# Two model blocks on one core: the scheduler's simulation is exchanged, and with it the order of every engine

## The chip, the cores and the metric

The kernel runs on one core of a Trainium2 chip. The metric is the device time of one execution in microseconds (us). Runs of this kernel scatter by about 0.2%. Engines are named as in the profile: PE is TensorE (PEld its weight loads), DVE is VectorE, ACT is ScalarE, POOL is GpSimd, SP is the engine that issues the loads.

## What is computed

Two transformer-like blocks on 512 tokens of width 1024, in float32. The first block (one layer) mixes by three branches: gated linear attention (GLA, 4 heads, chunked), a causal convolution, and attention in a window of 128 tokens with sinks (8 heads); then an FFN with a convolution. The second block has two layers, each with top-128 sparse attention (8 heads), an HGRN recurrence (4 heads), two gates and an FFN. Cut to the second block's mix:

```python
for l in range(DEPTH_2):
    h = rmsnorm_2(x, norm_mix[l])
    proj = h @ w_in[l]
    aq, ak, av, iq, ik, iw, hq, hf, hi, hg, ga, gb = jnp.split(proj, split_points, axis=-1)
    ...
    y_attn = dsa_attention(aq, ak, av, iq, ik, iw)     # scores of an indexer, top 128, softmax over these
    ...
    o = hgrn2_chunked(q_h, k_in, v_h, log_f)           # S_t = diag(f_t) S_{t-1} + k_t v_t^T
    ...
    merged = jax.nn.sigmoid(ga) * (y_attn @ w_proj_attn[l]) + jax.nn.sigmoid(gb) * (y_hgrn @ w_proj_hgrn[l])
    x = x + merged @ w_out[l]
    h = rmsnorm_2(x, norm_ffn[l])
    g, u = jnp.split(h @ w_ffn_in[l], 2, axis=-1)
    x = x + (jax.nn.silu(g) * u) @ w_ffn_out[l]
```

## The kernel before, in words

Activations lie with features on the 128 partitions and the 512 tokens along the row. A projection (`project`, L184) multiplies one 128-column tile of a weight with all eight tiles of the input: each float32 product is made of three matmuls of high and low parts (L193 low weight, L194 low input, L195 both high), so a projection of 1024 inputs is 24 matmuls of 512 columns into one PSUM bank. `project_tokens` (L156) does the same with tokens on the partitions (L168 to L170). The weights come through `weights` (L133): SP loads 512 KB into `wraw` (three buffers), ACT rounds the high part (`whi`, L149), and DVE or POOL subtracts it (`wlo`, L152).

The second block's mix (`second_mix`, L957) first does the sparse attention (`dsa`, L828): an indexer's scores, for query blocks 1 to 3 a selection of the 128 best by 16 rounds of MAX8 and MATCH_REPLACE8 on DVE (L885, L886), normalised and rotated keys and queries (`rotated`, L818, whose last multiplication is L825, followed by transposes on PE at L239 and, for queries, two copies at L249), and then `attend` (L915) for four query blocks of 128 tokens, eight heads each. A head is: scores on PE (L925, up to 512 columns), bias and minimum on DVE (L927), exp on ACT (L929), up to four transposes on PE (L933), a copy on ACT (L935), up to four matmuls with the values on PE (L937). At the end of a block the output is normalised (L941) and transposed. The scores and transposes use PSUM banks of lane "a"; that lane has two, and one of them holds the output `o` of the query block. Behind the attention in program order come four HGRN heads (`hgrn_head`, L468), each with three projections and seven levels in which DVE (L493, L497) and POOL (L494, L495) take turns and PE multiplies small blocks (L509), and then the two merges (`merge`, L677), whose projections need gates and the mixed outputs. At most two gates are made ahead of the first merge.

No order is written out by hand beyond that of the program. A scheduler takes the whole traced program, simulates the engines, and lets each engine take, at the simulated time at which it is free, the ready instruction of highest priority; weights and PSUM evictions are marked as of high priority. The order that comes out is fixed in the program: on the chip each engine works through its list and waits at semaphores. The scheduler has two simulations to choose from; the default is used before.

## Time and profile before

| | |
|---|---|
| median of 3 runs | 2590.12 us (2587.59 to 2593.46) |
| profiled execution | 2592.11 us |
| its span, first to last instruction | 2590.3 us |
| mean granted clock of PE | 0.990 |
| PE busy | 2504.4 us (97%) |
| DVE, ACT, POOL busy | 1362.4, 1011.7, 769.8 us |
| read from HBM | 213.5 MB, 83 GB/s over the span |

PE's busy time is that of its matmuls, which overlap one another in the pipeline: the mean duration of one 512-column matmul is about 0.39 us, but a run of them goes on at one per 0.227 us. A float32 matmul without the split shows as two rows. The granted clock is 1.00 (2.4 GHz) or 0.50 (1.2 GHz) at any moment; a stretch shows the mean.

### The profile page before, as it was taken

How to read it: one execution, taken by the hardware profiler on the slowest of the kernel's cores; microseconds unless marked ns; L12 is line 12 of the kernel's file. 1: busy time of each engine (PE TensorE's matmuls, PEld its weight loads, DVE VectorE, ACT ScalarE, POOL GpSimd, SP SyncE). 2: the span in 40 equal slices, each digit the busy share in tenths (PEclk: the TensorE clock that was granted, in tenths of full speed). 3: DMA queues.
4: the chain of work that ended last, by engine and by line, in shares of the span. 5: the costliest groups of instructions: out<-in, count | busy, mean ns of one | idle time of the engine just before them, and what ended most of it. 6: DMA issues, size and time to landing. Idle time of an engine off the chain costs nothing.

```text
span 2590.3 us, 31616 instructions
## 1 busy us (share of the span) xinstructions
PE 2504.4 (97%) x11742; PEld 2047.2 (79%) x11742; DVE 1362.4 (53%) x2568; ACT 1011.7 (39%) x1830; POOL 769.8 (30%) x676
## 2 busy tenths in 40 slices
PE   9999999999999998899999999999798999999999
PEld 7877888888888766777888888887677788888887
DVE  4675222477764677765244444336877523444432
ACT  5633333444443344453343333334355333433322
POOL 4234334511101333643361110013465335211100
PEclk9999999999999999999999999999899999999999
DMA  4112233322233222111332223332211123222233
GB/s 136 58 60 82 87 97 98 102 98 98 97 95 96 76 74 73 42 37 59 94 99 98 97 94 95 94 98 66 73 42 40 34 96 101 96 94 96 97 108 88
DMA packets 67434, 217.66 MB, mean 84 GB/s; under 512 B 7744, under 2 KB 8640, under 8 KB 67280
## 3 DMA queue, kind: packets, MB, share of 16 engines
q1 hardware_dynamic: 67280, 215.65, 26.1%
q8 instruction: 92, 1.51, 0.2%
q14 instruction: 62, 0.51, 0.1%
HBM read 213.52 MB, written 2.10 MB: 83 GB/s over the span
## 4 chain that ended last, share of the span: by engine, by line
PE 80%; DVE 14%; POOL 3%; issue 2%; ACT 1%; DMA 0%; SPq 0%; DVEq 0%; POOLq 0%; ACTq 0%
PE mm L194 23%; PE mm L195 23%; PE mm L193 23%; DVE score L886 2%; DVE m L885 2%; PE at L925 1%; PE at L937 1%; PE at L239 1%; DVE wlo L152 1%; POOL hG L495 1%; PE mm L169 1%; PE mm L170 1%; PE mm L168 1%; DVE rsq_w L231 1%; PE at L933 1%
## 5 line engine op out<-in xcount | busy, mean ns | idle before, releaser
L149 ACT CAST whi<-wraw 128x512 fp32r<-128x512 f32 (+3 forms) x824 | 502.3, 610 | 1139.9 <-PE mm L195 950.4
L193 PE MATMUL mm<-xh,wlo 128*128 128x512 f32 x1920 | 759.0, 395 | 0.0
L194 PE MATMUL mm<-xl,whi 128*128 128x512 f32 x1920 | 758.2, 395 | 0.0
L195 PE MATMUL mm<-xh,whi 128*128 128x512 f32 x1920 | 755.5, 393 | 0.0
L152 DVE TENSOR_TENSOR wlo<-wraw,whi 128x512 fp32r<-128x512 f32 (+1 forms) x529 | 385.2, 728 | 458.5 <-ACT whi L149 455.4
L152 POOL TENSOR_TENSOR wlo<-wraw,whi 128x512 fp32r<-128x512 f32 (+2 forms) x295 | 381.4, 1293 | 760.5 <-ACT whi L149 689.6
L195 PEld LDWEIGHTS mm<-xh,whi 128*128 128x128 f32 x1920 | 361.8, 188 | 74.5 <-issue 1.9
L194 PEld LDWEIGHTS mm<-xl,whi 128*128 128x128 f32 x1920 | 361.9, 188 | 73.5 <-issue 1.7
L193 PEld LDWEIGHTS mm<-xh,wlo 128*128 128x128 f32 x1920 | 361.8, 188 | 72.9 <-issue 1.2
L193 PE MATMUL mm<-acth,wlo 128*128 128x512 f32 x528 | 205.4, 389 | 0.0
L194 PE MATMUL mm<-actl,whi 128*128 128x512 f32 x528 | 205.4, 389 | 0.0
L195 PE MATMUL mm<-acth,whi 128*128 128x512 f32 x528 | 205.4, 389 | 0.0
L733 POOL TENSOR_TENSOR fg<-fg,rstd 128x512 f32<-128x512 f32 x44 | 56.7, 1289 | 425.6 <-ACT fg L732 425.6
L168 PE MATMUL mm<-wlo,xh 128*128 128x512 f32 (+2 forms) x384 | 147.0, 383 | 17.3 <-POOL wlo L152 9.2
L169 PE MATMUL mm<-whi,xl 128*128 128x512 f32 (+2 forms) x384 | 145.2, 378 | 0.2 <-DVE xl L288 0.2
L170 PE MATMUL mm<-whi,xh 128*128 128x512 f32 (+2 forms) x384 | 145.1, 379 | 0.0
L202 DVE TENSOR_TENSOR gate<-mm,rstd 128x512 f32<-128x512 f32 x56 | 38.7, 691 | 165.2 <-PE mm L195 164.3
L277 POOL TENSOR_TENSOR acc<-acc,sq 128x512 f32<-128x512 f32 x39 | 58.9, 1509 | 199.2 <-ACT sq L274 198.3
L194 PEld LDWEIGHTS mm<-actl,whi 128*128 128x128 f32 x528 | 99.1, 188 | 20.8
L193 PEld LDWEIGHTS mm<-acth,wlo 128*128 128x128 f32 x528 | 99.1, 188 | 20.6
L195 PEld LDWEIGHTS mm<-acth,whi 128*128 128x128 f32 x528 | 99.1, 188 | 20.4
L168 PEld LDWEIGHTS mm<-wlo,xh 128*128 128x128 f32 x384 | 73.4, 191 | 36.1 <-POOL wlo L152 11.7
(352 smaller groups left out, 3333.1 us busy)
## 6 DMA issues: line engine op xcount, KB each, us to landing
wraw<-in_w_ffn_in SPq DMA_DIRECT2D x88, 512.0 KB, 3.3
wraw<-in_w_gate SPq DMA_DIRECT2D x56, 512.0 KB, 3.3
wraw<-in_w_in SPq DMA_DIRECT2D x52, 512.0 KB, 3.3
wraw<-in_w_up SPq DMA_DIRECT2D x44, 512.0 KB, 3.2
wraw<-in_w_tok SPq DMA_DIRECT2D x32, 512.0 KB, 3.2
wraw<-in_w_ffn_out SPq DMA_DIRECT2D x32, 512.0 KB, 3.6
wraw<-in_w_down SPq DMA_DIRECT2D x16, 512.0 KB, 3.6
wraw<-in_w_po SPq DMA_DIRECT2D x32, 256.0 KB, 2.6
```

The source lines that it names most:

```text
L149: nc.scalar.copy(wh, raw[:, k:k + m, :])
L152: eng.tensor_tensor(wl, raw[:, k:k + m, :], wh.bitcast(F32), op=OP.subtract)
L168: nc.tensor.matmul(ps[t][:, 0:w], xh, wl, start=i == 0, stop=False)
L169: nc.tensor.matmul(ps[t][:, 0:w], xl, wh, start=False, stop=False)
L170: nc.tensor.matmul(ps[t][:, 0:w], xh, wh, start=False, stop=i == KD - 1)
L193: nc.tensor.matmul(ps, wl, xh, start=i == 0, stop=False)
L194: nc.tensor.matmul(ps, wh, xl, start=False, stop=False)
L195: nc.tensor.matmul(ps, wh, xh, start=False, stop=i == n - 1)
L277: (nc.vector if d % 2 and len(acc) > 1 else nc.gpsimd).tensor_tensor(a, a, sq, op=OP.add)
L733: nc.gpsimd.tensor_tensor(g, g, self.rstd, op=OP.mult)
L885: nc.vector.max(m8, sc[:, 0:w])
L886: nc.vector.match_replace(sc[:, 0:w], m8, sc[:, 0:w], TAKEN)
```

## The change

One argument of the context in which the program is traced. With it the scheduler takes ready and free times from the toolchain's other simulation of the engines, and nothing else is different: the operations, the tiles, the buffers and the priorities stay.

```diff
@@ -1097,7 +1097,7 @@
     out = nc.dram_tensor("out_0", (KD, P, T), F32, kind="ExternalOutput").ap()
-    with tile.TileContext(nc) as tc:
+    with tile.TileContext(nc, schedule_with_timeline_sim=True) as tc:
         model(tc, A, out)
```

Of PE's 10,973 instructions, DVE's 2,474, POOL's 681 and SP's 470, the same number of each line stand in both orders; ACT has 30 table loads where it had 36. What moves shows best at the following places.

PE in the last query block of the first layer's attention in the second block. Before, projections (L193 to L195) and HGRN steps (L474, L488) stand between the steps of the heads:

```order
L933 MATMUL at<-csts,aL 128x128 x4
L195 MATMUL mm<-xh,whi 128x512
L193 MATMUL mm<-xh,wlo 128x512
L194 MATMUL mm<-xl,whi 128x512
L195 MATMUL mm<-xh,whi 128x512
L937 MATMUL at<-av,aPT 128x64 x4
L925 MATMUL at<-kT,qT 128x512
L474 MATMUL at<-hq,hk 128x128 x4
L488 MATMUL at<-lvx,ones 128x256
L193 MATMUL mm<-xh,wlo 128x512
L194 MATMUL mm<-xl,whi 128x512
```

At the same place now, from the end of query block 2 on:

```order
L937 MATMUL at<-av,aPT 128x64 x3
L239 MATMUL at<-csts,aon 128x128 x4
L239 MATMUL at<-csts,aro 128x128 x4
L925 MATMUL at<-kT,qT 128x512
L933 MATMUL at<-csts,aL 128x128 x4
L937 MATMUL at<-av,aPT 128x64 x4
L925 MATMUL at<-kT,qT 128x512
```

The three rows L925, L933 and L937 stand there eight times in a row, once for each head, and nothing else between them. From the third head of query block 1 to the end of block 3 PE's list holds 280 instructions and no projection; before, the longest such run is 25 instructions. The second layer has the same run of 280, and the first block's mix has one of 92, where the old order has at most 22.

DVE at the rotated keys in the same layer (aro; akss and rsq are the keys' normalisation, score and m the selection, tabS the rotation's table). Before, the multiplications L825 stand after 16 rounds of the selection at 256 columns and 13 at 384:

```order
L886 MATCH_REPLACE score<-m_7701,score 128x384
L232 SCALAR_TENSOR_TENSOR rsq_w<-rsq_w,rsq_y 128x32
L801 TENSOR_TENSOR rope_8019<-akx,tabS 128x8x32
L885 MAX m_7704<-score 128x8
L233 SCALAR_TENSOR_TENSOR rsq_y<-rsq_w,rsq_y 128x32
L886 MATCH_REPLACE score<-m_7704,score 128x384
L825 TENSOR_TENSOR aro<-aro,rsq_y 128x512
L885 MAX m_7707<-score 128x8
```

Now they stand together, after 16 rounds at 256 columns and 2 at 384:

```order
L886 MATCH_REPLACE score<-m_7671,score 128x384
L233 SCALAR_TENSOR_TENSOR rsq_y<-rsq_w,rsq_y 128x32
L885 MAX m_7674<-score 128x8
L825 TENSOR_TENSOR aro<-aro,rsq_y 128x512 x4
L886 MATCH_REPLACE score<-m_7674,score 128x384
```

At the first attention head of this layer, PE's list has six projection matmuls ahead of the first scores and eleven behind in the old order, 24 and 29 in the new one; they read like the rows of L193 to L195 above. Moved here with the rest: DVE's multiplications stand 11 selection rounds earlier, and the rounds passed over come behind them.

## Rows read from the trace of the kernel before

**Rows 1.** Busy time of each engine, and the chain that ended last, of the page.

```profile
PE 2504.4 (97%) x11742; PEld 2047.2 (79%) x11742; DVE 1362.4 (53%) x2568; ACT 1011.7 (39%) x1830; POOL 769.8 (30%) x676
PE 80%; DVE 14%; POOL 3%; issue 2%; ACT 1%; DMA 0%; SPq 0%; DVEq 0%; POOLq 0%; ACTq 0%
```

**Rows 2.** Stretches: us, then busy us (instructions) of PE, PEld, DVE, ACT, POOL; clock, DMA.

```profile
30.00:230.00 200.00, 190.75 (x1059) 157.55 (x1060) 119.38 (x323) 97.05 (x217) 69.32 (x60) 1.00 0.20 64
230.00:890.00 660.00, 657.31 (x2926) 543.94 (x2925) 345.54 (x517) 259.57 (x418) 180.08 (x137) 1.00 0.30 96
890.00:1200.00 310.00, 278.34 (x1473) 218.41 (x1472) 234.81 (x534) 139.78 (x288) 143.59 (x149) 0.98 0.16 51
1735.00:2045.00 310.00, 279.94 (x1425) 221.39 (x1426) 222.96 (x511) 135.02 (x279) 148.75 (x154) 0.94 0.17 54
```

**Rows 3.** Whom PE waited for, 890 to 1200 us: us in total, times, longest.

```profile
PE at L239 <- DVE aro L825: 13.6, 4, 8.3
PE mm L168 <- POOL wlo L152: 4.9, 3, 2.1
```

**Rows 4.** Groups by line and form, 890 to 1200 us: busy us, mean ns; idle before.

```profile
L885 DVE MAX8 m<-score 128x8 f32<-128x384 f32 x16 | 8.8, 553 | 0.2
L886 DVE MATCH_REPLACE8 score<-m,score 128x384 f32<-128x384 f32 x16 | 8.6, 540 | 0.0
```

**Rows 5.** One head of query block 3 in order of time: start us, us, engine, line.

```profile
1159.57 1.08 PE L925 MATMUL at<-kT,qT 128*128 128x512 f32 x2
1160.69 0.69 DVE L927 CUSTOM_DVE_ANT_0 aL<-at,score 128x512 f32<-128x512 f32 x1 [1.06 <-PE at L925]
1161.42 0.72 ACT L929 ACTIVATE aL<-aL,anm 128x512 f32<-128x512 f32 x1 [1.81 <-DVE anm L927]
1162.29 0.42 PEld L933 LDWEIGHTS at<-csts,aL 128*128 128x128 f32 x4 [0.23 <-ACT aL L929]
1162.32 0.63 PE L933 MATMUL at<-csts,aL 128*128 128x128 f32 x4
1162.98 0.59 ACT L935 COPY aPT<-at 128x512 f32<-128x512 f32 x1 [0.74 <-PE at L933]
1163.62 0.97 PEld L937 LDWEIGHTS at<-av,aPT 128*128 128x128 f32 x8 [0.19 <-ACT aPT L935]
1163.71 1.01 PE L937 MATMUL at<-av,aPT 128*128 128x64 f32 x8
1164.56 0.65 PE L925 MATMUL at<-kT,qT 128*128 128x512 f32 x1
```

**Rows 6.** Groups by line and form, 890 to 1200 us: the same steps in query block 1.

```profile
L927 DVE CUSTOM_DVE_ANT_0 aL<-at,score 128x256 f32<-128x256 f32 x8 | 3.3, 417 | 2.4 <-PE at L925 2.4
L929 ACT ACTIVATE aL<-aL,anm 128x256 f32<-128x256 f32 x8 | 4.1, 510 | 13.8 <-DVE anm L927 13.8
L935 ACT COPY aPT<-at 128x256 f32<-128x256 f32 x8 | 3.0, 372 | 3.3 <-PE at L933 3.2
```

**Rows 7.** Groups by line and form, 890 to 1200 us: the next query.

```profile
L802 POOL TENSOR_TENSOR aro<-rope,rope 128x512 f32<-128x512 f32 x8 | 10.3, 1282 | 8.3 <-DVE rope L801 7.8 <-DVE rss L412 0.4
L825 DVE TENSOR_TENSOR aro<-aro,rsq_y 128x512 f32<-128x512 f32 x8 | 7.3, 918 | 1.9 <-POOL aro L802 1.9
```

**Rows 8.** Groups by line and form, 890 to 1200 us: POOL's two steps of an HGRN level.

```profile
L494 POOL TENSOR_TENSOR lvx<-hG,hk 128x256 f32<-128x256 f32 x24 | 22.4, 935 | 1.5
L495 POOL TENSOR_TENSOR hG<-hG,hf 128x256 f32<-128x256 f32 x24 | 18.9, 786 | 6.3 <-DVE hf L497 5.0 <-ACT aPT L935 0.4
```

**Rows 9.** Two stretches at the second layer's attention (columns as in rows 2), and PE's order.

```profile
2030.90:2041.10 10.20, 10.20 (x43) 8.26 (x42) 5.05 (x13) 2.41 (x5) 4.75 (x5) 0.50 0.00 0
2041.10:2051.30 10.20, 10.20 (x64) 8.11 (x62) 5.58 (x19) 4.22 (x10) 0.78 (x1) 1.00 0.16 53
...
2031.17 1.92 PE L937 MATMUL at<-av,aPT 128*128 128x64 f32 x8
2032.88 2.02 PE L925 MATMUL at<-kT,qT 128*128 128x512 f32 x2
```

## The prediction, made before the changed kernel ran

> **What bounds the kernel now.** I read the page's busy times and chain first, then the busy time of each engine by stage, then who TensorE waited for, and last single steps in order of time. TensorE is busy for 2504.4 of 2590.3 us, and 80% of the chain that ended last is its own work [rows 1]. So the time is TensorE's work plus its idle time plus what a lowered clock costs, and an order can only touch the last two. By stage [rows 2], the stretch 230 to 890 us, which holds the rest of the first mix and the whole first FFN, has 660 - 657.3 = 2.7 us of idle time. The two stretches that hold the second block's mixes have 310 - 278.3 = 31.7 us (first layer) and 310 - 279.9 = 30.1 us (second layer) at mean clocks of 0.98 and 0.94. The first block's attention and GLA (30 to 230 us) have 200 - 190.8 = 9.2 us. So about 71 of the 86 us of idle time lie in three stages, in which TensorE alternates between projections (L168 to L170, L193 to L195), which are always ready, and chains of small steps (attention, GLA, HGRN), which are not. There the order decides what TensorE has to do while a small step runs elsewhere.
>
> **What the change does not touch.** Every engine gets the same instructions, apart from 6 fewer table loads on ACT, an engine that is busy for 139.8 of 310 us in these stages [rows 2]; I count 0 for them, since projections run on TensorE beside them in the old order, and without that cover they would only make the tail below a little shorter. SP's queue loads the weights in nearly the old order. In the FFNs the order of TensorE's matmuls is the same and TensorE is full, so I count 0 there; the cover is the three weight buffers, and if it failed the idle time would show in the stretch 230 to 890.
>
> **What it moves, first part: projections go early.** In each second-block mix the waits for the rotated keys and queries (L239 on L825) cost 13.6 us, one of them 8.3 us [rows 3]. In the new order DVE reaches the four multiplications L825 of the keys after 18 rounds of the selection (L885, L886) where it was after 29; 11 rounds at 0.55 + 0.54 us [rows 4] are 12 us, more than the 8.3 us wait, so I count it as gone. The selection rounds come later and are late next, but TensorE then has runs of up to 29 projection matmuls between two steps of the first attention heads, where the longest run had 17. What I expect to stay are the waits for weights (L168 on L152), 4.9 us behind POOL [rows 3], say 8 us with the smaller ones. So this part gives 31.7 - 8 = 24 us in the first layer and 22 us in the second. With the long waits go the stretches at half clock that they lead to: 0.02 x 310 = 6 us and 0.06 x 310 = 19 us [rows 2] at most, but half clock costs nothing while TensorE is idle, so I take half: 3 and 10 us.
>
> **Second part: nothing is left for the end.** These projections are a fixed number, and the new order uses them up during the first ten of 32 attention heads (4 query blocks of 8 heads). From there to the end of the attention TensorE's order holds 280 instructions without one projection matmul: 22 attention heads (6 of query block 1, 8 each of blocks 2 and 3) and two HGRN heads. The longest such run in the old order is 25. Within a head the steps follow each other strictly, since one of the lane's two PSUM banks holds the output and scores and transposes take turns in the other: scores (L925), DVE (L927), exp on ACT (L929), transposes (L933), copy on ACT (L935), values (L937), next scores. A head of block 3 shows it [rows 5]: the scores start at 1159.57 and end at 1160.65, the transposes' first load stands at 1162.29, they end at 1162.95, the values' load stands at 1163.62, and the next scores start at 1164.56. So a head takes 5.0 us at the least, and TensorE has no work of it in 1162.29 - 1160.65 = 1.64 us and in 1163.62 - 1162.95 = 0.67 us, 2.31 us in all. Now projections fill this; in the new order nothing does. For block 1 the DVE, exp and copy rows are 0.27, 0.21 and 0.22 us shorter [rows 6], which leaves 1.61 us; block 2 lies between, 1.96 us. That makes 6 x 1.61 + 8 x 1.96 + 8 x 2.31 = 43.8 us. Between query blocks the next query must be rotated and copied: POOL 1.28 us and DVE 0.92 us [rows 7], ahead of them two DVE multiplications and the normalisation, behind them two copies; 5.2 us each time as an estimate, and 2 us at the end until the first output projection has its operand: 12.4 us. The HGRN heads work both ways. Their 94 small matmuls, at 1.01 us for four like L937 [rows 5], are 23 us that fit into these gaps; but their own ping-pong of POOL and DVE takes 6 x (0.935 + 0.786) = 10.3 us in its levels alone [rows 8], some 19 us with what stands ahead and behind, while 4.5 attention heads would take 13 to 17 us, so it stretches the tail by about 10. At full clock the tail thus adds 43.8 + 12.4 - 23 + 10 = 43 us in each layer.
>
> **The clock in the tail.** The nearest thing to this tail is the stretch 2030.9 to 2041.1 us: attention and HGRN matmuls with 5 projection matmuls among its 43 rows. TensorE counts as busy in all of it, and the granted clock is 0.50, its lower level of 1.2 GHz; in the 10.2 us behind it, with the same kind of work and 15 projection matmuls, it is 1.00 [rows 9]. A chip that lets its clock fall there, beside full occupancy by small matmuls, will hardly keep it up where they have gaps. At half clock the scores take 2.02 us and the values 1.92 us [rows 9] against 1.08 and 1.01 [rows 5]; with the transposes a head of block 3 is 2.3 us longer, one of block 2 1.7, one of block 1 1.15: 38.7 us for 22 heads. The HGRN matmuls double to 46 us and no longer fit, some 15 us; transitions add 3; the stretching of 10 us is swallowed. So at half clock throughout, the tail adds 43 + 38.7 + 15 + 3 - 10 = 90 us. I take 80, since it begins right behind dense projections at the full clock; the ends are 43 and 90.
>
> The Trainium skill (TensorE: Matmul & The Clock Gate, section on HAM oscillation) warns of long idle gaps of TensorE alone; gaps of 2 us with small matmuls between them would by it leave the clock at 2.4 GHz, and the sum would be the first rival's, below. The trace speaks against it with the row just named.
>
> **The first mix** has the same in small: at its end 92 instructions without a projection (one softmax block of four rounds, one GLA head), where the old order has at most 22. By count that is a third of the other tails, 14 us at full clock and 30 at half; of the old 9.2 us some 6 go. I take 18 - 6 = 12 us.
>
> **Sum.** First layer 80 - 24 - 3 = 53, second layer 80 - 22 - 10 = 48, first mix 12: 113 us. The profiled execution took 2592.1 us, 2.0 us above the median of the runs shown (2590.1), which changes nothing here: 2592 + 113 = 2705 us.
>
> **Rivals.**
> First, the clock stays up in the tails. For it: in 2041.1 to 2051.3 attention runs at 1.00 [rows 9]. Against it: the stretch before, and that no projections stand in the tails. Then the tails add 43 us: 43 - 27 = 16, 43 - 32 = 11, first mix 8; 35 us, 2627 us.
> Second, the other side: the early gain is larger than the tail. That needs heads that overlap, the next one's scores running beside this one's softmax, so that of the 2.31 us only a part is bare and the HGRN matmuls fill that. The gain is 27 + 32 us less 8 to 12 us in the first mix, so it decides at about 24 us of tail in each layer; at 10 us the time is 2592 - 17 - 22 + 8 = 2561 us. Against it: scores, transposes and values of one head stand in a row in the new order, and TensorE takes its matmuls in that order.
> Third, the first half goes wrong as well: DVE has the selections of 512 columns, the weights' subtractions and the HGRN steps at the same time as the first heads, and the early projections wait for their weights. DVE is busy for 234.8 of 310 us of this stage [rows 2], so the gain of 24 and 22 us would go and not come: 2705 + 46 = 2751 us.
> That the flag does nothing is ruled out: the orders differ.
>
> **Numbers.** Forecast (tails at or near half clock) 68%, first rival 17%, third 10%, second 3%, tails and gains that cancel 2%. The forecast's own ends are 2680 and 2730 us; the first rival's bounds reach down to 2610 us where the HGRN heads do not stretch its tail. The range 2620 to 2765 us takes in the first and the third rival and leaves out the rest of the low end and anything worse than the third. A measurement here can tell about 0.2% (5 us): faster by more 0.03, within it 0.02, slower 0.95.
>
> **What would show it.** Right, if in the changed kernel the two layers' mixes have over 40 us of idle time each at the attention's end, with L933 waiting for the exp and L937 for the copy about 20 times in each, a granted clock near 0.5 there, the 8 us wait for L825 gone, and the FFN stretches unchanged. The clock row is wrong if the tails show 1.00; the cycle is wrong if a head of block 3 takes much other than 5.0 us (7.3 at half clock). The whole is wrong if the tails' idle time is under 24 us each, or if the FFNs begin to show gaps.

## The result, and the profile after

The changed kernel takes 2722.41 us (median of 4 runs, 2721.54 to 2726.73), the kernel before beside it 2588.86 us (2587.22 to 2593.46): a ratio of 1.0516, 95% interval 1.0498 to 1.0534, 133.6 us slower. The forecast was 2705 us. The profiled execution took 2722.77 us with a span of 2721.0, which is 130.7 us more than the span of before.

The page of the changed kernel: busy time by engine, the granted clock by fortieths of the span, and the chain that ended last. They answer to [rows 1].

```profile
PE 2567.5 (94%) x11742; PEld 2100.1 (77%) x11742; DVE 1364.4 (50%) x2568; ACT 1006.0 (37%) x1824; POOL 779.8 (29%) x676
PEclk9999999999999999965999999999997689999999
PE 84%; DVE 9%; ACT 3%; issue 2%; POOL 1%; DMA 1%; SPq 0%; DVEq 0%; ACTq 0%; POOLq 0%
```

TensorE has the same 11742 matmuls and is busy for 63 us more, so about half of the loss lies within its busy time and not in idle time. The clock falls most at two places, and the stretches of the changed kernel (columns as in [rows 2]) show what they are:

```profile
204.00:236.00 32.00, 22.27 (x151) 19.28 (x150) 22.94 (x81) 14.74 (x41) 5.92 (x5) 0.91 0.07 21
236.00:895.00 659.00, 659.00 (x2934) 547.55 (x2935) 347.91 (x517) 260.40 (x419) 183.32 (x138) 1.00 0.30 95
895.00:1135.00 240.00, 219.10 (x1050) 177.98 (x1049) 176.64 (x376) 98.99 (x196) 115.52 (x114) 0.96 0.21 71
1135.00:1284.00 149.00, 103.55 (x454) 72.47 (x453) 65.22 (x175) 39.41 (x95) 32.58 (x37) 0.66 0.01 3
...
1815.00:2048.00 233.00, 217.20 (x1063) 176.94 (x1062) 171.89 (x363) 101.78 (x200) 123.81 (x119) 0.99 0.22 73
2048.00:2197.00 149.00, 101.73 (x452) 72.01 (x450) 65.66 (x172) 38.60 (x93) 32.40 (x37) 0.67 0.01 2
```

The stretches 1135 to 1284 and 2048 to 2197 us are the two tails without a projection: 149 us each, TensorE idle for 45 and 47 us, the mean clock 0.66 and 0.67. The stretch 204 to 236 us is the small one of the first mix. From 236 to 895 us TensorE is never idle, where it had 2.7 us of idle time from 230 to 890 us [rows 2].

Inside the first tail the clock stands at 0.50 without a break for 81.9 us, through all of query block 3, and TensorE is never idle for longer than 1.8 us at a time there; in layer 2 the same lasts 75 us (2124.7 to 2199.7 us):

```profile
1206.50:1288.40 81.90, 53.89 (x156) 33.34 (x156) 13.46 (x39) 16.86 (x40) 1.26 (x1) 0.50 0.01 2
```

In the tail, TensorE waits where the prediction said (waits of TensorE, 1135 to 1284 us: us in total, times, longest), and in the stretch ahead of it (895 to 1135 us, below the dots) the waits for L825 [rows 3] have given way to another:

```profile
PE at L933 <- ACT aL L929: 21.9, 16, 1.7
PE at L937 <- ACT aPT L935: 9.3, 14, 0.7
...
PE mm L168 <- DVE wlo L152: 9.7, 1, 9.7
...
PE at L239 <- DVE aro L825: 0.9, 1, 0.9
```

One head of query block 3 in order of time in the tail, to be laid beside [rows 5]:

```profile
1251.88 2.02 PE L925 MATMUL at<-kT,qT 128*128 128x512 f32 x2
1255.65 1.12 PE L933 MATMUL at<-csts,aL 128*128 128x128 f32 x4 [1.75 <-ACT aL L929]
1257.50 1.97 PE L937 MATMUL at<-av,aPT 128*128 128x64 f32 x8 [0.73 <-ACT aPT L935]
1259.26 1.17 PE L925 MATMUL at<-kT,qT 128*128 128x512 f32 x1
```

From scores to scores 1259.26 - 1251.88 = 7.38 us, with the matmuls at nearly twice the duration of [rows 5] and two bare gaps. From the first scores of block 3 to its eighth it is 51.3 us in either layer, 7.33 us a head.

I measure a mix from the start of its first token projection (L168) to the start of the first matmul of its output projection. In us of the profiled executions, before and after: first mix 457.9 and 468.6 (+10.8), layer 1 446.5 and 518.5 (+72.0), layer 2 452.1 and 507.8 (+55.7), 138.5 in all. Each of the three stretches from there to the FFN's second projection is 2.4 us shorter (287.0 to 287.2 before, 284.7 now), and so the sum comes to about 131 us.

### The profile page after: what moved, and what is told of

It is laid out like the page before. It is cut to its first block, busy times and chain, and to the rows that moved or that the text cites. A ratio compares the mean times of both kernels' runs of the same rounds, so it can differ in the third digit from the quotient of the medians.

```text
span 2721.0 us, 31584 instructions
## 1 busy us (share of the span) xinstructions
PE 2567.5 (94%) x11742; PEld 2100.1 (77%) x11742; DVE 1364.4 (50%) x2568; ACT 1006.0 (37%) x1824; POOL 779.8 (29%) x676
## 4 chain that ended last, share of the span: by engine, by line
PE 84%; DVE 9%; ACT 3%; issue 2%; POOL 1%; DMA 1%; SPq 0%; DVEq 0%; ACTq 0%; POOLq 0%
PE mm L193 23%; PE mm L195 23%; PE mm L194 23%; PE mm L168 2%; PE mm L169 2%; PE mm L170 2%; PE at L937 2%; PE at L925 2%; DVE score L886 1%; DVE m L885 1%; PE at L933 1%; ACT aL L929 1%; PE at L239 1%; POOL hG L495 1%; DVE aL L927 1%
## 5 line engine op out<-in xcount | busy, mean ns | idle before, releaser
L193 PE MATMUL mm<-xh,wlo 128*128 128x512 f32 x1920 | 757.5, 395 | 4.9 <-POOL wlo L152 1.9
L195 PE MATMUL mm<-xh,whi 128*128 128x512 f32 x1920 | 753.9, 393 | 0.0
L152 DVE TENSOR_TENSOR wlo<-wraw,whi 128x512 fp32r<-128x512 f32 (+1 forms) x529 | 390.8, 739 | 512.4 <-ACT whi L149 509.2
L152 POOL TENSOR_TENSOR wlo<-wraw,whi 128x512 fp32r<-128x512 f32 (+2 forms) x295 | 387.5, 1315 | 751.5 <-ACT whi L149 716.0
L193 PEld LDWEIGHTS mm<-xh,wlo 128*128 128x128 f32 x1920 | 362.8, 189 | 81.2 <-DVE wlo L152 2.4
L195 PEld LDWEIGHTS mm<-xh,whi 128*128 128x128 f32 x1920 | 362.6, 189 | 75.6 <-issue 0.5
L193 PE MATMUL mm<-acth,wlo 128*128 128x512 f32 x528 | 205.4, 389 | 0.0
L195 PE MATMUL mm<-acth,whi 128*128 128x512 f32 x528 | 205.4, 389 | 0.0
L168 PE MATMUL mm<-wlo,xh 128*128 128x512 f32 (+2 forms) x384 | 147.7, 389 | 28.3 <-DVE wlo L152 20.2
L202 DVE TENSOR_TENSOR gate<-mm,rstd 128x512 f32<-128x512 f32 x56 | 38.7, 691 | 159.8 <-PE mm L195 159.8
L193 PEld LDWEIGHTS mm<-acth,wlo 128*128 128x128 f32 x528 | 99.1, 188 | 20.7
L195 PEld LDWEIGHTS mm<-acth,whi 128*128 128x128 f32 x528 | 99.1, 188 | 20.4
L168 PEld LDWEIGHTS mm<-wlo,xh 128*128 128x128 f32 x384 | 74.4, 194 | 45.2 <-DVE wlo L152 21.4
```

The source lines that it names most:

```text
L152: eng.tensor_tensor(wl, raw[:, k:k + m, :], wh.bitcast(F32), op=OP.subtract)
L168: nc.tensor.matmul(ps[t][:, 0:w], xh, wl, start=i == 0, stop=False)
L193: nc.tensor.matmul(ps, wl, xh, start=i == 0, stop=False)
L195: nc.tensor.matmul(ps, wh, xh, start=False, stop=i == n - 1)
```

## The experiments

My theory: the early projections leave the late attention heads bare; each bare head is a serial chain, since scores and transposes take turns in one PSUM bank; and the clock falls in it. Each of the three can be taken away. The ratios are to the kernel before, run beside each on the same chip (medians of 2587.8 to 2591.7 us).

| run | us (lowest to highest) | ratio to before, 95% interval |
|---|---|---|
| pace | 2637.14 (2634.7 to 2638.8) | 1.0179 (1.0162 to 1.0196) |
| pace2 | 2614.62 (2613.2 to 2616.85) | 1.0095 (1.008 to 1.011) |
| pace2b | 2663.33 (2659.42 to 2670.25) | 1.0288 (1.0267 to 1.031) |
| warm0 | 2742.05 (2738.23 to 2746.23) | 1.0585 (1.0569 to 1.0601) |
| warm | 2704.72 (2703.82 to 2707.45) | 1.0442 (1.0427 to 1.0458) |
| lowsP | 2731.37 (2730.2 to 2735.59) | 1.0546 (1.0531 to 1.0562) |
| h1a3 | 2607.73 (2604.24 to 2610.59) | 1.0067 (1.0052 to 1.0082) |
| b_h1a3 | 2621.94 (2619.89 to 2623.97) | 1.0122 (1.0107 to 1.0137) |
| x3 | 2599.04 (2595.86 to 2606.81) | 1.0045 (1.003 to 1.006) |
| b_x3 | 2602.63 (2597.94 to 2604.82) | 1.0049 (1.0037 to 1.0061) |
| x3p | 2617.13 (2611.75 to 2619.5) | 1.0107 (1.0093 to 1.0121) |
| y4 | 2627.01 (2624.52 to 2627.33) | 1.014 (1.0123 to 1.0157) |

### Projections held back: pace, pace2, pace2b

In each second mix the projection matmuls behind the attention (in pace the first 336, those of the HGRN heads and of two gates) get an ordering edge each to a step of a head, which only the scheduler sees: both run on TensorE, so no semaphore is added. A list gives how many are released behind each head's scores and transposes.

```diff
+                for a, b, s, e in ((wl, xh, i == 0, False), (wh, xl, False, False), (wh, xh, False, i == n - 1)):
+                    m = nc.tensor.matmul(ps, a, b, start=s, stop=e)
+                    if self.quota:
+                        k, self.quota[0][1] = self.quota[0][0], self.quota[0][1] - 1
+                        if not self.quota[0][1]:
+                            self.quota.pop(0)
+                        self.tc.add_manual_dep(m.ins, self.marks[k].ins.name, mybir.DependencyInfo(
+                            mybir.DependencyClass.NoSync, mybir.DependencyReason.DATA), reason="pace")
...
+        self.quota = [[2 * (8 * i + j) + s, ((5, 7, 8, 9), (3, 3, 3, 4))[s][i]] for i in range(4) for j in range(8) for s in range(2)]
```

> The new scheduler, but in both second-block mixes the 336 projection matmuls behind the attention are held back on TensorE: after the scores of each head 5, 7, 8 or 9 of them (query block 0 to 3) and after its transposes 3 or 4 may go, by an order between instructions of one engine, without a semaphore. Theory (projections go early and leave the tail bare): both runs without projections vanish, each layer's mix loses most of the 83 us that its tail adds, the granted clock stays at 1.00 there, and the time is 2560 to 2620 us. Rival (the loss is spread over waits that the new order makes everywhere, for weights and in the queues of DVE and ACT): less than half of the 131 us comes back, over 2660 us.

Measured 2637.14 us: 85 of the 133 us came back, between the two expectations. Stretches of this run show what stayed:

```profile
1104.30:1118.30 14.00, 9.35 (x42) 7.11 (x42) 13.30 (x25) 4.09 (x10) 9.17 (x11) 0.68 0.06 23
1118.30:1165.00 46.70, 42.87 (x247) 34.04 (x246) 26.26 (x63) 19.27 (x40) 16.93 (x19) 0.99 0.11 35
1165.00:1179.10 14.10, 8.74 (x50) 7.00 (x49) 11.85 (x23) 2.45 (x7) 10.55 (x13) 0.71 0.11 38
```

Within query block 2, the second row, the heads now run at a clock of 0.99 (0.98 in block 3, 1179.1 to 1243 us). The transitions around it, to block 2 and to block 3, have no projection, are idle for 4.7 and 5.4 us of 14 and fall to 0.68 and 0.71: an even dose leaves nothing for them. So pace2 takes the numbers (`PACE`, 64 for each layer, from 11, 2, 5, 4 on) from the order of before, in which the last transposes of a block are followed by 21, 10 and 23 projection matmuls, and pace2b does that in the first layer alone.

```diff
+        self.quota = [[k, n] for k, n in enumerate(PACE[l]) if n]
```

> The changed scheduler with every projection of the two second-block mixes released after the same scores or transposes as in the order of the kernel before, head by head, so that the transitions between query blocks (20 to 23 projections each) are covered too. If the loss is the lack of projections at the late heads and nothing else, the loss of 72 and 56 us in the two mixes goes: 2580 to 2605 us, first mix still 11 us longer. Rival: the new order of the other operations (norm, HGRN, splits of weights) costs by itself, as the 47 us that the first pacing left over would have it: 2620 us or more.

> As the run pace2, with only the mix of layer 1 held back. If the two losses are separate, only layer 1's 72 us come back and layer 2 stays 56 us longer: 2640 to 2665 us. Rival: what layer 1 spends early layer 2 or the feed-forward gets back, so the two are coupled: outside 2635 to 2670 us.

pace2 came to 2614.62 us, between its two expectations again: 108 of 133 us are back. The mixes take 461.9 and 457.0 us, so 57 of 72 and 51 of 56 us are recovered, and the first mix, which was left alone, is still 11 us longer (468.8). What is left of layer 1 is partly the new wait for weights (L172 is L168 here), and the heads' waits for exp (L943 is L933) that projections do not cover, where the kernel before has one such wait of 2.2 us:

```profile
PE at L943 <- ACT aL L939: 7.7, 10, 1.5
PE mm L172 <- DVE wlo L156: 6.9, 1, 6.9
```

pace2b came to 2663.33 us as expected: layer 1 falls to 462.2 us and layer 2 stays at 502.7. The two losses are separate.

### The clock by itself: warm0, warm

In warm, each head of query blocks 1 to 3 issues six 512-column matmuls behind its scores and two behind its transposes, into a PSUM bank that nobody reads: 8 x 24 heads x 2 layers = 384 matmuls of more work. They keep TensorE active and add no step to the head's chain. warm0 is the control: the same bank taken and the same steps tied together, with `NFILL = (0, 0)`, none of these matmuls.

```diff
+NFILL = (6, 2)
...
-                nc.tensor.matmul(ps[:, 0:w], qT[i][hd % 2][:, hd // 2, :], kT[hd // 2][:, 0:w], start=True, stop=True)
+                m = nc.tensor.matmul(ps[:, 0:w], qT[i][hd % 2][:, hd // 2, :], kT[hd // 2][:, 0:w], start=True, stop=True)
+                m = self.fill(dm, X[0][0], NFILL[0], m)
```

> The changed kernel with one PSUM bank of four taken away from the projections during the attention, and the steps of each head tied in their order; the control of the next run. Both theories: the tails stay, about 150 us each at a clock near 0.5, and the time is 2715 to 2740 us.

> As the control, and in query blocks 1 to 3 each head has 6 matmuls of 512 columns behind its scores and 2 behind its transposes, whose result nobody reads: 192 more matmuls a layer, all in gaps. Theory (half of what the tail adds is the clock): the clock in the tails rises to 1.00, a head of block 3 takes 5.0 to 5.4 us in place of 7.4, a tail some 115 us in place of 149, and the time falls by 50 to 75 us against the control although TensorE does more. Rival (the chain through DVE and ACT alone sets the tail, the clock is a by-product): a head stays at 7 us or grows, and the time is that of the control or up to 30 us more.

warm0 is 20 us slower than the changed kernel, somewhat above its expectation. warm is 37 us faster than warm0 in spite of 384 matmuls more; 50 to 75 us were expected. The two tails of warm0, then of warm:

```profile
1133.50:1287.90 154.40, 106.60 (x471) 74.63 (x469) 69.89 (x179) 39.76 (x97) 31.99 (x39) 0.65 0.01 3
2058.30:2212.10 153.80, 108.53 (x453) 76.65 (x451) 64.81 (x170) 38.94 (x95) 31.73 (x37) 0.62 0.01 2
```

```profile
1143.50:1279.20 135.70, 116.53 (x629) 86.02 (x627) 65.57 (x162) 37.57 (x92) 32.15 (x37) 0.94 0.01 4
2045.40:2179.40 134.00, 115.39 (x627) 85.28 (x625) 63.14 (x158) 37.46 (x91) 30.97 (x35) 0.95 0.01 3
```

The clock rises from 0.65 and 0.62 to 0.94 and 0.95, and the tails, with 22 bare heads each in warm and 23 and 22 in warm0, shorten by 18.7 and 19.8 us. Not all of that arrives: layer 1's mix is only 5 us shorter than warm0's (514.8 against 519.9 us), since the stretch ahead of its tail is 13 us longer (263.1 against 249.9 us), and layer 2's is 26 us shorter (494.2 against 520.2). The added matmuls change the scheduler's order there too, so the tails tell what the clock is worth and the 37 us only roughly. A head of block 3 in warm in order of time (L940 scores, L949 transposes, L954 values, L115 the added ones):

```profile
1246.51 1.08 PE L940 MATMUL at<-kT,qT 128*128 128x512 f32 x2
1247.02 1.95 PE L115 MATMUL mm<-xh 128*128 128x512 f32 x6
1249.29 0.66 PE L949 MATMUL at<-csts,aL 128*128 128x128 f32 x4 [0.32 <-ACT aL L945]
...
1250.62 1.10 PE L954 MATMUL at<-av,aPT 128*128 128x64 f32 x8 [0.21 <-ACT aPT L952]
1251.56 1.08 PE L940 MATMUL at<-kT,qT 128*128 128x512 f32 x2
```

It takes 1251.56 - 1246.51 = 5.05 us with eight matmuls more, where the changed kernel takes 7.38, and warm0's heads of block 3 take 7.27 to 7.38 too. So half clock costs a late head 2.3 us, and what is left at full clock is the serial chain, which extra work does not shorten.

### The new wait for weights: lowsP

The 9.7 us wait of L168 is for a low part that DVE computes. Here the token projections' low parts of the second mixes go to POOL alone, instead of to POOL twice and DVE once in turn.

```diff
         with self.on("a"):
+            self.lows = [nc.gpsimd]
             yattn = self.dsa(l, X)
+            self.mixing()
```

> The changed kernel, but the low parts of the weights of the token projections in the second block's mixes are subtracted on POOL alone, where one of three stood in the queue of DVE. Theory (the early gain fell short because the projections waited for a low part queued on DVE behind the selection and the rotation): the waits of L168 for DVE, 9.7 and 5.9 us, go, and the time is 2700 to 2714 us. Rival (POOL, which also rotates and fills, is then as late): no change within 5 us, or slower.

2731.37 us, as the rival had it. The wait moves to POOL and to the rotated keys, for which POOL multiplies (waits of TensorE of this run, 895 to 1150 us):

```profile
PE mm L168 <- POOL wlo L152: 4.2, 2, 3.4
PE at L239 <- DVE aro L825: 3.9, 1, 3.9
```

The mixes take 522.1 and 518.2 us, 4 and 10 us more than without it. The rival's reason, that POOL is as late, is only part of it. Ahead of its tail layer 1 is 3 us shorter than in the changed kernel (250.8 against 253.8 us), layer 2 is 4 us longer, and the tails are longer, 154 and 155 us against 148, at clocks of 0.61 and 0.63. So handing the low parts to POOL gains at most 3 us ahead of a tail, and the rest of the difference comes with the order that the edit brings along; why the tails grow was not taken apart.

### The serial chain by itself: h1a3, b_h1a3

Eight PSUM banks are shared out as four for projections, two for lane "h" (norms, GLA, HGRN) and two for lane "a" (attention). With three for the attention, one head's scores need not wait until the copy has emptied the bank of the head before. The control has the same banks on the scheduler of before.

```diff
-    BANKS = {"h": 2, "a": 2}
+    BANKS = {"h": 1, "a": 3}
```

> The changed scheduler with three PSUM banks for the attention instead of two, and one for the norms and HGRN instead of two, so that the scores of a head need not wait for the copy of the transposed weights of the head before. If the bare heads are one serial chain because scores and transposes take turns in one bank, two heads overlap and each tail falls from 149 us to 80 to 115 us; with what the missing bank costs elsewhere 2630 to 2700 us. Rival: the chain is held by the engines beside TensorE (exponential, copy, reduction): tails of 140 us or more and 2700 us or more.

> Control: the same banks on the scheduler of before. There the projections already cover the heads' chain, so the third bank can give nothing, and the missing one of the norms and HGRN costs: 2590 to 2640 us. Its distance to before is what the bank costs in the run h1a3 outside the tails.

h1a3 takes 2607.73 us, 115 us less than the changed kernel, and b_h1a3 2621.94, 32 more than the kernel before. The tails of h1a3 as stretches, and two of its heads in order of time:

```profile
1146.00:1231.00 85.00, 65.95 (x425) 51.60 (x423) 59.77 (x149) 33.56 (x75) 32.35 (x38) 0.92 0.02 6
1994.00:2080.00 86.00, 67.89 (x424) 52.24 (x422) 58.74 (x147) 33.29 (x74) 33.00 (x38) 0.90 0.01 4
```

```profile
1203.08 0.66 PE L933 MATMUL at<-csts,aL 128*128 128x128 f32 x4 [0.34 <-ACT aL L929]
1203.57 1.02 PE L925 MATMUL at<-kT,qT 128*128 128x512 f32 x2
...
1205.38 1.00 PE L937 MATMUL at<-av,aPT 128*128 128x64 f32 x8
1206.72 0.66 PE L933 MATMUL at<-csts,aL 128*128 128x128 f32 x4 [0.33 <-ACT aL L929]
1207.21 1.02 PE L925 MATMUL at<-kT,qT 128*128 128x512 f32 x2
```

TensorE's order still has a run of 259 instructions without a projection in each layer, but the scores of the next head now stand between transposes and values. Between these two heads 1207.21 - 1203.57 = 3.64 us pass; over block 3 of this layer it is 3.2 to 7.2 us, 4.6 on average against 7.33. The tails take 85 and 86 us at clocks of 0.92 and 0.90. Part of that is that fewer heads are bare: the run holds the scores of 16 heads, where that of the changed kernel holds 22. The mixes are 449.1 and 445.2 us, level with before (446.5, 452.1). The first mix pays for the missing bank: 484.8 us against 468.6.

What matters most: with these banks the same change of the scheduler is a gain, 2621.94 to 2607.73 us, 14 us or 0.5%, with ranges that don't touch. It is a gain over the old order with these banks, not over the kernel before, which is faster than both.

### Towards a version that beats both: x3, b_x3, x3p, y4

x3 lends the third bank only for the second mixes, where it holds a block's outputs (L920); elsewhere lane "h" has it. b_x3 is the same on the scheduler of before, x3p also holds the first mix's projections back by the order of before, and y4 keeps the last 72 of the 336 projection matmuls of each second mix for the heads of blocks 1 to 3 (the last line of the diff).

```diff
-    BANKS = {"h": 2, "a": 2}
+    BANKS = {"h": 1, "a": 2, "x": 1}
+    lent, turn = False, True
...
-    def at(self, shape=None):
-        return self.pp.tile(shape or [P, T], F32, name="at", tag="p" + self.lane, bufs=self.BANKS[self.lane])
+    def at(self, shape=None, lane=None):
+        lane = lane or self.lane
+        if lane == "h" and not self.lent:
+            self.turn = not self.turn
+            lane = "hx"[self.turn]
+        return self.pp.tile(shape or [P, T], F32, name="at", tag="p" + lane, bufs=self.BANKS[lane])
...
-            o = self.at([P, 8, 64])
+            o = self.at([P, 8, 64], "x")
...
+            self.quota = [[0, 264]] + [[2 * j + s, 2 - s] for j in range(8, 32) for s in range(2)]
```

> The changed scheduler with the third attention bank only lent: it holds a block's outputs in the second mixes and belongs to the norms and to the first mix elsewhere. From the runs with three banks throughout: their second mixes took 449 and 445 us (changed scheduler as it is: 519 and 508), so 70 and 62 us come back, and the first mix, which lost a bank there, keeps its 469 us: 2585 to 2600 us, level with the kernel before. Rival: HGRN with one bank beside the heads is what costs, and the first mix is not: 2600 to 2615 us.

> The lent bank on the scheduler of before. Its heads are covered by projections, so the third bank has nothing to shorten, and HGRN has one bank less beside them: 2588 to 2615 us. If it comes below 2585 us, the bank is worth something by itself, and x3 and x3p owe their time to it and not to the two parts together.

x3 takes 2599.04 us, as expected, and b_x3 2602.63: between these two the ranges overlap, and the change makes no difference that can be told. Its first mix still loses (468.0 against 458.7 us), and its second mixes are shorter by 4.5 and 3 us (453.6 and 449.2 against 458.1 and 452.2). So, each time against the old order with the same banks, the change loses 133.6 us with the banks as they are, nothing with a lent third one, and gains 14 us with a moved one.

> As x3, with the first mix's projections released as in the order of before (in that stage alone). If the first mix's 11 us come from its 32 us without projections, they return: 9 to 13 us less than x3, 2573 to 2591 us, faster than before if x3 is level. Rival: the pacing moves other waits into the stage (as it did in the second mixes, where 19 of 128 us stayed): within 4 us of x3.

18 us slower than x3 instead of 9 to 13 faster. The first mix takes 485.8 us. The first 100 us of it, of x3p and of x3:

```profile
30.00:130.00 100.00, 93.53 (x505) 76.90 (x504) 40.73 (x140) 57.10 (x131) 27.20 (x27) 0.96 0.21 67
```

```profile
30.00:130.00 100.00, 98.13 (x498) 81.70 (x497) 41.63 (x116) 50.30 (x99) 39.83 (x34) 0.97 0.25 83
```

Holding back makes TensorE idle for 6.5 us here against 1.9, and a stretch of 28.9 us without projections (224.8 to 253.7 us) still stands at the end: it is put off, not removed. My 11 us for this stage by such a simple cure were wrong.

> As x3, with the last 72 projections that each second mix can have before its outputs kept for the heads of query blocks 1 to 3, two released after a head's scores and one after its transposes; the 264 before them run as early as the scheduler likes. In x3 TensorE idles 16 us in each stretch without projections (90 and 86 us) and the clock falls to 0.95 and 0.85 there. If three projections a head (1.2 us) cover what is left of each head's chain, 10 to 16 us of each mix come back: 2567 to 2582 us, faster than both kernels. Rival: the same idle time moves to the early part, where the kept projections are missing: within 6 us of x3, 2593 to 2605 us.

2627.01 us, 28 us slower than x3. Three projection matmuls in a run take 0.7 us (3 x 0.227), not the 1.2 us that I counted, so they cover less. The held-back matmuls begin with the gate of the last HGRN head. The last level of this head on L520 (L509 in the changed kernel) ends at 1242.2 us, 33 us behind the last attention step (1209.4), where in x3 the two end together (1215.6 and 1216.8). That the held gate is what delays the head was not tested. Two stretches nearly without projections, one between blocks and one behind that head:

```profile
1158.00:1174.00 16.00, 10.47 (x48) 8.45 (x47) 12.68 (x26) 3.86 (x10) 11.42 (x12) 0.64 0.00 0
1243.00:1259.00 16.00, 6.38 (x37) 5.14 (x37) 7.38 (x22) 2.42 (x4) 0.00 (x0) 0.76 0.06 16
```

No version was faster than the kernel before; the nearest is x3 at 1.0045.

## Why the prediction was right, and where a term was off

**Direction and cause** were right. The tails take 149 us each; work of the same kind in h1a3 is counted busy for 65.95 us in 425 rows and 67.89 in 424, which for 454 and 452 rows makes 70 and 72 us, an estimate that still has a clock of 0.9 in it and fewer heads among its rows. So the tails add about 79 and 77 us, where I took 80. Taking away any one cause moves the time the way it should: projections in the tails (pace2, -108), overlapping heads (h1a3, -115), the clock (warm against warm0, -37 with added work, where 50 to 75 were expected). L933 waits for the exp 16 and 18 times in the two tails and L937 for the copy 14 and 15 times, where I had said about 20 each.

**The clock.** I took the tails at or near half clock; the mean is 0.66, since it falls to 0.50 for good only at 1206.5 us, 71 us into the tail. (My terms for the 22 heads at half clock add up to 38.9 us, not 38.7, which changes nothing.) The head of block 3, forecast at 5.0 us at full and 7.3 at half clock, measured 5.05 (in warm) and 7.38. The first rival (clock stays up, 2627 us) fell with the rows at 0.66. The page that I cited for it, in the Trainium skill (TensorE: Matmul & The Clock Gate), has a further section, A second HAM failure mode: psum-queue depth-cycling, by which short idle times between groups of matmuls are enough to make the clock oscillate. The trace agrees with it in part: in the 81.9 us at 0.50 no idle time is longer than 1.8 us, but the clock stays down there and does not oscillate; the rule on long gaps, which would have kept it up, did not hold there. The first fall in the tail, at 1165.5 us, came in a longer idle time of 3.6 us.

**The mis-sized term is the first part, "projections go early".** I gave it 24 + 3 us in layer 1 and 22 + 10 in layer 2. Measured, it is the tail's cost less the mix's loss: 79 - 72 = 7 us and 77 - 56 = 21 us. Ahead of the tail TensorE is idle for 240 - 219.1 = 20.9 us and 233 - 217.2 = 15.8 us, against 31.7 and 30.1 us in [rows 2]: 11 and 14 us gained, not 24 and 22. The term that I had too small is "What I expect to stay are the waits for weights, say 8 us": the wait for L825 went as forecast (it is 0.9 us now ahead of the tail), but at the same place one of 9.7 us for a low part on DVE came, 5.9 in layer 2. What remains, 4 us lost in layer 1 and 7 gained in layer 2, I put down to the clock, and no run shows it alone: layer 1 has 0.96 ahead of the tail, against 0.98 over its whole stretch in [rows 2], and layer 2 has 0.99 against 0.94. The third rival has its result in part: it would have had the gain of 24 and 22 us lost whole, 2751 us, and about half was. With 7 and 21 in place of 27 and 32 the forecast's own sum is 2592 + 73 + 59 + 12 = 2736 us; less the 5 us by which tails and first mix were overrated and the 7 us that the three stretches to the FFNs' second projections gave, 2724. That is an account and no test, since the 7 and 21 come out of the mixes.

**The other points.** First mix 12 us: 10.8 measured. The stretches to the FFNs' second projections, counted at 0, gained 2.4 us each: TensorE was idle for 1.2 to 1.4 us in each of them before and is not now; the other 1 us was not taken apart. The second rival needed heads that overlap, and TensorE's order excluded it, as written. h1a3 agrees with its condition: where heads overlap, TensorE is idle for 19 and 18 us in the tails, under the 24 us from which that rival decides, and with these banks the change gains. The 24 us themselves rest on the early gain of 27 and 32 us, which came out as 7 and 21.

**What stays open.** pace2 repeats the old number of projections behind every step and is still 15 us and 5 us slower in its two mixes than before. It has the wait of 6.9 us for weights and 7.7 us of waits for the exp, where the kernel before has waits for L825; the sum was not taken apart. That the first mix loses its 11 us in its bare 32 us was not shown either, since x3p only moved the bare stretch. Why this simulation lets the projections go earlier than the default one was not looked into.

## What to carry to other kernels

A list scheduler that takes whatever is ready can spend the independent work early, as it did here with one of its two simulations, and the dependent chains then run bare; look in the new order for the longest run without the filler matmuls, take the cycle of the chain inside it from the trace, and price it at full and at half clock. Whether an order is good depends on the buffers it may use: one more PSUM bank, which let two heads overlap, turned a loss of 5% into nothing or a small gain against the old order with the same banks. Count a wait as gained only after asking what else the same engine has queued at that place, since the next one is often right behind it.

## What the runs showed of the hardware

DVE and POOL hold each other up around the wait of 9.7 us. TensorE, DVE and POOL of the changed kernel there, in order of time by engine:

```profile
980.25 0.79 PE L168 MATMUL mm<-wlo,xh 128*128 128x512 f32 x1 [9.69 <-DVE wlo L152]
...
972.32 1.16 DVE L231 TENSOR_TENSOR rsq_w<-akss,rsq_y 128x32 f32<-128x32 f32 x1
976.18 0.17 DVE L231 TENSOR_TENSOR rsq_w<-akss,rsq_y 128x32 f32<-128x32 f32 x1
978.40 1.80 DVE L152 TENSOR_TENSOR wlo<-wraw,whi 128x512 fp32r<-128x512 f32 x1
...
972.17 1.26 POOL L802 TENSOR_TENSOR aro<-rope,rope 128x512 f32<-128x512 f32 x1 [0.54 <-DVE rope L801]
978.39 1.26 POOL L152 TENSOR_TENSOR wlo<-wraw,whi 128x512 fp32r<-128x512 f32 x1
```

The same 32-column multiplication L231 takes 0.17 us when POOL is idle and 1.16 when it starts 0.15 us behind an instruction of POOL; it then ends at 973.48, 0.05 us after POOL's end at 973.43. The low part L152 took 1.80 us beside POOL's 1.26, against its mean of 0.74. Seven of DVE's instructions between 969 and 981 us take longer than alone, by about 6.5 us together (an estimate from the durations of the same instructions where POOL is idle), and the low part for which TensorE waits is the last of them. This is not what the change brought: in the kernel before, at least nine are held so between 961 and 981 us, the same multiplication for instance at

```profile
963.98 1.08 DVE L231 TENSOR_TENSOR rsq_w<-akss,rsq_y 128x32 f32<-128x32 f32 x1
```

So it lengthens the wait, and what is new is that the low part stands behind these instructions in DVE's list. No run took the holding away by itself.

By the Trainium skill (SBUF — State Buffer, section Who interferes with whom), a DVE instruction with two inputs in SBUF and a GpSimd instruction that reads SBUF use one shared port pair, and the one that comes second is blocked until the first is done. The trace agrees: L231 ends with POOL's instruction, and L152 0.55 us after it (978.40 + 1.80 against 978.39 + 1.26). One of the seven, L229, reads a single tile and takes 1.24 us, which this sentence on two inputs does not cover.

The granted clock is the other point: the first tails of warm0 and warm ran at 0.65 and at 0.94, and the difference in what TensorE did was eight matmuls of 512 columns a head whose results nothing uses.
